# One store of 8 KB blocks for all phases of a hybrid decoder layer, bulk transfers on a second queue

## The chip, the core and the metric

One core of a Trainium2 chip runs the whole layer. The metric is the device time of one execution in microseconds (us).

## The reference

One layer over 2048 tokens of width 1024, float32. Cut to what matters:

```python
u = h @ w_in
q, k, v, xr, gr = jnp.split(u, splits, axis=-1)
att = sliding_window_sink_attention(q, k, v, attn_sinks)   # window 128
xr = causal_dwconv(xr, rnn_conv_w, rnn_conv_b)
rec = rg_lru(xr, gate_a_w, gate_a_b, gate_x_w, gate_x_b, lru_lambda)
rec = rec * jax.nn.gelu(gr, approximate=True)
mix = jnp.concatenate([att, rec], axis=-1) @ w_out
h = layer_norm(ALPHA * h + mix, ln1_g, ln1_b)
gate, val = jnp.split(h @ w_up, 2, axis=-1)               # 1024 -> 2 x 3072
gate = causal_dwconv(gate, conv_w, conv_b)
ffn = (jax.nn.gelu(gate, approximate=True) * val) @ w_down
ple = jax.nn.sigmoid(h @ ple_gate_w + ple_gate_b) * (p @ ple_proj)
h = layer_norm(ALPHA * h + ffn + ple, ln2_g, ln2_b)
```

## The kernel before

Every product is made of three: each operand is split into a high and a low part in a 32-bit matmul type (`split_sb`, lines 111 to 113: ACT copies the high part, DVE subtracts), and `mm3` (lines 129 to 132) issues hi x hi, hi x lo and lo x hi. So nearly all time of PE has lines 130 to 132. Weights come as units of 128 x 1024 words (512 KB) through `wst` (3 buffers) and are split into `wb` (8 buffers of half a unit).

*Phase A* (lines 230 to 572) runs over 4 chunks of 512 tokens. x of a chunk is split into four tiles of the pool `t1` (4 buffers of 8 KB a partition). The first stage (`first_stage`) makes 14 units of 128 columns from it; then come RG-LRU, attention, and the mixing with W_OUT into four tiles of 128 tokens, norm 1 (`layer_norm`), and PE transposes that give h as `hh_`, `hl_` (again the four buffers of `t1`) and `hf` (pool `t2`). The gating of the per-layer embedding (lines 542 to 571) then makes, in two halves `dh` of 512 columns, four tiles of 24 matmuls each with h, and DVE adds the result into `rs`, which is stored to DRAM as `rsd`. The next chunk's x needs the buffers that gating still reads.

*Between the phases.* Two chunks form a half `s2` for the FFN. Up uses a scheme with seven products in place of eight, on operands B11, T2, B21, T1, T3, T4, B22 (`HX`), each 4 x 128 x 512 in two parts, 2 MB. An even chunk stores its h as B11, B21 and `hfd`; an odd chunk stores B22, and `combine` (lines 518 to 532) reads `hfd` back, makes T1 to T4 by four adds and four splits for each of four slices, and stores 8 pieces of 256 KB a slice. All four calls stand in the first half of gating, one behind each token tile. All these pass through DRAM (`hxd`).

*Up* (lines 581 to 670, twice) closes phase A's pools, opens its own, and loads all seven operands (line 595). Then 24 feature tiles `ft` run `begin`, `middle`, `end`, with the order of PE written out by hand; the results gc go to DRAM (`gd`), two feature tiles a block. *Down* (lines 672 to 722, twice) opens its own pools again and runs over two chunks; for each of 12 steps `kp` it loads `graw`, splits it into `gb`, and adds 2 x 4 token tiles x 6 matmuls into eight PSUM banks; after the last step come the sums with `rsd`, norm 2 and the store of four token tiles.

*What sets the order.* A scheduler orders the instructions of each engine, except where `order(...)` or the manual schedule of up pins them. Pools opened with `scoped` (`reuse_waits="tile"`) share memory between phases, and a tile of a new phase waits for the old tiles at its place. Every DMA is issued on SP's queue. Where the tiles of phase A start follows from what was allocated before them: `t1`, `t2` and pt tiles lie 96 bytes past a multiple of 128, the attention's and gates' temporaries 32 past; all of up and down and `wb` lie at a multiple of 128.

## Time and profile before

| what | value |
|---|---|
| median of 3 runs | 2465.29 us (2464.33 to 2469.13) |
| the profiled execution, its own time | 2466.69 us |
| span in the profile | 2465.0 us |
| PE busy | 2329.7 us, 95%, 10156 matmuls |
| DVE, ACT, POOL busy | 67%, 44%, 6% |
| phase A; up, down of half 0; up, down of half 1 | to 938; 1422, 1690; 2182, 2465 us |
| DMA | 340.08 MB, nearly all on one queue |

A view by windows gives, for a stretch of the span, each engine's busy time and count of instructions, the granted clock of TensorE as a share of its full level (2.4 GHz; the lower level is 1.2), and what the DMA engines did. Matmuls overlap, so a count in a window says more than a mean duration. The waits say how long PE stood still and what released it.

### The profile page before, as it was taken

How to read it: one execution, taken by the hardware profiler on the slowest of the kernel's cores; microseconds unless marked ns; L12 is line 12 of the kernel's file. 1: busy time of each engine (PE TensorE's matmuls, PEld its weight loads, DVE VectorE, ACT ScalarE, POOL GpSimd, SP SyncE). 2: the span in 40 equal slices, each digit the busy share in tenths (PEclk: the TensorE clock that was granted, in tenths of full speed). 3: DMA queues.
4: the chain of work that ended last, by engine and by line, in shares of the span. 5: the costliest groups of instructions: out<-in, count | busy, mean ns of one | idle time of the engine just before them, and what ended most of it. 6: DMA issues, size and time to landing. Idle time of an engine off the chain costs nothing. (4 is left out here: it accounts for less than half of the span.)

```text
span 2465.0 us, 28138 instructions
## 1 busy us (share of the span) xinstructions
PE 2329.7 (95%) x10156; PEld 1882.5 (76%) x10156; DVE 1657.6 (67%) x2728; ACT 1084.1 (44%) x2028; POOL 145.7 (6%) x258
## 2 busy tenths in 40 slices
PE   9999999799989987999999999996999999999997
PEld 7777777577777765888888878884788888878886
DVE  7975788678668773877777743635677777753634
ACT  7643665466446452444444433331344444433331
POOL 1300030003002100000000000000000000000000
PEclk9999999899999998999999999998999999999999
DMA  4236325732542287232222264635422222264551
GB/s 160 90 131 236 111 69 194 249 111 77 195 156 94 94 282 298 94 91 81 86 77 86 94 227 140 220 122 197 179 83 88 86 77 79 92 214 141 182 173 60
DMA packets 99308, 340.08 MB, mean 138 GB/s; under 512 B 10464, under 2 KB 10592, under 8 KB 93536
## 3 DMA queue, kind: packets, MB, share of 16 engines
q1 hardware_dynamic: 99168, 338.28, 40.4%
q8 instruction: 80, 1.31, 0.2%
q14 instruction: 60, 0.49, 0.1%
HBM read 262.74 MB, written 75.50 MB: 137 GB/s over the span
## 5 line engine op out<-in xcount | busy, mean ns | idle before, releaser
L112 ACT CAST wb<-wst 128x512 fp32r<-128x512 f32 x640 | 390.6, 621 | 741.5 <-PE sc L132 286.5
L113 DVE TENSOR_TENSOR wb<-wst,wb 128x512 fp32r<-128x512 f32 x640 | 433.5, 686 | 322.9 <-ACT wb L112 321.7
L131 PE MATMUL b<-T,wb 128*128 128x512 f32 x576 | 225.4, 391 | 2.8 <-DMA T<-hxT 2.8
L130 PE MATMUL b<-T,wb 128*128 128x512 f32 x576 | 225.7, 392 | 2.2 <-DVE u L642 1.6
L132 PE MATMUL b<-T,wb 128*128 128x512 f32 x576 | 224.9, 391 | 0.4 <-DVE wb L113 0.4
L601 DVE SCALAR_TENSOR_TENSOR gc<-xb,prm,gc 128x512 f32<-128x512 f32 x192 | 144.1, 750 | 109.9 <-issue 84.4
L130 PE MATMUL a<-B,wb 128*128 128x512 f32 x384 | 151.8, 395 | 29.6 <-DMA B<-hxB 29.6
L112 ACT CAST wb<-s 128x512 fp32r<-128x512 f32 x144 | 89.4, 621 | 195.0 <-PE a L132 92.6
L131 PE MATMUL a<-B,wb 128*128 128x512 f32 x384 | 152.4, 397 | 6.8 <-DMA B<-hxB 6.8
L132 PE MATMUL a<-B,wb 128*128 128x512 f32 x384 | 151.6, 395 | 0.0
L113 DVE TENSOR_TENSOR wb<-s,wb 128x512 fp32r<-128x512 f32 x144 | 99.3, 689 | 62.1 <-ACT wb L112 62.1
L131 PEld LDWEIGHTS b<-T,wb 128*128 128x128 f32 x576 | 108.7, 189 | 27.1 <-DMA T<-hxT 4.9
L130 PEld LDWEIGHTS b<-T,wb 128*128 128x128 f32 x576 | 108.8, 189 | 26.6 <-DVE u L642 2.7
L132 PEld LDWEIGHTS b<-T,wb 128*128 128x128 f32 x576 | 108.6, 189 | 23.3 <-DVE wb L113 0.8
L130 PE MATMUL acc<-wb,t1h 128*128 128x512 f32 x256 | 104.1, 415 | 20.2 <-ACT wb L112 14.2
L130 PEld LDWEIGHTS a<-B,wb 128*128 128x128 f32 x384 | 73.5, 191 | 46.0 <-issue 30.6
L132 PE MATMUL acc<-wb,t1l 128*128 128x512 f32 x256 | 103.6, 406 | 1.2 <-DVE t1l L88 1.2
L131 PE MATMUL acc<-wb,t1h 128*128 128x512 f32 x256 | 104.5, 409 | 0.0
L130 PE MATMUL acc<-t1h,wb 128*128 128x512 f32 x192 | 81.2, 423 | 23.4 <-ACT wb L112 23.1
L132 PE MATMUL a<-t1h,wb 128*128 128x512 f32 x256 | 102.7, 401 | 0.0
L130 PE MATMUL a<-t1h,wb 128*128 128x512 f32 x256 | 102.6, 401 | 0.0
L131 PE MATMUL a<-t1l,wb 128*128 128x512 f32 x256 | 102.4, 400 | 0.0
(246 smaller groups left out, 5564.1 us busy)
## 6 DMA issues: line engine op xcount, KB each, us to landing
wst<-in_w_dram SPq DMA_DIRECT2D x319, 512.0 KB, 3.7
gd<-gc SPq DMA_DIRECT2D x48, 512.0 KB, 4.8
...
T<-hxT SPq DMA_DIRECT2D x16, 1024.0 KB, 19.6
...
```

What stands on the lines that cost most here:

```text
L112: ACT.copy(hi, src)
L113: (eng or DVE).tensor_tensor(lo, src, f(hi), ALU.subtract)
L130: order(PE.matmul(o, ah, bh, start=first, stop=False, skip_group_check=more), after)
L131: PE.matmul(o, ah, bl, start=False, stop=False, skip_group_check=more)
L132: return PE.matmul(o, al, bh, start=False, stop=last, skip_group_check=more)
L601: DVE.scalar_tensor_tensor(gc, xb[:, o:o + T], pc(C_FW + 3 * ft + t_), gc, ALU.mult, ALU.add)
```

## The change

All tiles of 8 KB a partition (k and v, gate weights, x, m, q, h, hf, pt, the operands of up, graw, gb) come from one pool `h` of 13 blocks, and no pool is closed before the end. Temporaries share tags over all phases (`xc` 3, `xd` 1, `r` 4, others 2), rows with a conv tail come from `row()` (2 buffers). `epst` is 9 columns wide and the pools are so ordered that every TensorE operand starts at a multiple of 128 bytes. The stores of `hxd`, `hfd` and `rsd` and the loads of `hx` go to POOL's queue. The seven operands of up(0) are asked for in chunk 3: B11 after the last scores, T2 and B21 after mixing, T1, T3, T4 after gating's first half, B22 at its end, B22's low part into four pieces in `pch`/`pcl`. Those of up(1) are asked for in down(0)'s second chunk, four after step 6 and three at the end. Two combines stand in each half of gating. The x loads of the next chunk are ordered after the transposes. Up stores each 512-column half of gc by itself, with a row each; `graw` holds two steps. In down the last two steps run token tile by token tile; norms of tiles 0 and 1 (all four in the last chunk) follow their sums at once, those of 2 and 3 are put off into the next phase (`later`). The diff, cut to its core:

```diff
+XB = T + 8
+N8 = 13
...
+    h_p = ctx.enter_context(tc.tile_pool(name="h", bufs=N8))
+    tmp = ctx.enter_context(tc.tile_pool(name="tmp", bufs=2))
+    xb_p = ctx.enter_context(tc.tile_pool(name="xb", bufs=2))
...
+    def h8(name, shape, dt=F32R):
+        return h_p.tile(shape, dt, tag="h", name=nm(name))
...
-    epst = cst.tile([P, 1], F32, tag="epst", name="epst")
+    epst = cst.tile([P, 9], F32, tag="epst", name="epst")[:, 0:1]
...
+    def load_hx(s2, names, earlier):
+        for n in names:
+            hx[s2][n] = []
+            for m in range(2):
+                if (n, m) == (HX[-1], 1):
+                    ts = [tm(("pch", "pcl")[k % 2], F32R) for k in range(4)]
+                    for k in range(4):
+                        order(POOL.dma_start(f(ts[k]), hxd[s2][n][:, m, k, :]), earlier)
+                else:
+                    t = h8(n, [P, 4, T])
+                    order(POOL.dma_start(f(t), hxd[s2][n][:, m]), earlier)
+                    ts = [t[:, k, :] for k in range(4)]
+                hx[s2][n].append(ts)
...
-            SP.dma_start(st.rearrange("p (k t) -> p k t", k=2), xt[c, :, 2 * u:2 * u + 2, :])
+            order(SP.dma_start(st.rearrange("p (k t) -> p k t", k=2), xt[c, :, 2 * u:2 * u + 2, :]), have_h)
...
+        if c == NCH - 1:
+            load_hx(0, HX[:1], last_scores)
+            load_hx(0, HX[1:3], [mixed])
...
-                    SP.dma_start(hxd[s2][n][:, m], f(t))
-                SP.dma_start(hfd[s2][:, 4 * u:4 * u + 4], hf[u])
+                    POOL.dma_start(hxd[s2][n][:, m], f(t))
+                POOL.dma_start(hfd[s2][:, 4 * u:4 * u + 4], hf[u])
...
-                SP.dma_start(hxd[s2][n][:, 0, kt, :], f(hi))
-                SP.dma_start(hxd[s2][n][:, 1, kt, :], f(lo))
+                POOL.dma_start(hxd[s2][n][:, 0, kt, :], f(hi))
+                POOL.dma_start(hxd[s2][n][:, 1, kt, :], f(lo))
...
-                    SP.dma_start(rsd[c * NTOK + t_], rs[t_])
-                elif c % 2:
-                    combine(t_)
+                    POOL.dma_start(rsd[c * NTOK + t_], rs[t_])
+                if c % 2 and t_ % 2 != dh:
+                    combine(2 * dh + t_ // 2)
+            if dh == 0:
+                half = [gated]
+        if c == NCH - 1:
+            load_hx(0, HX[3:6], half)
+            load_hx(0, HX[6:], [gated])
...
-            for n in HX:
-                for m in range(2):
-                    SP.dma_start(f(hx[n][:, m]), hxd[s2][n][:, m])
...
-                SP.dma_start(gd[s2][ft // 2][:, ft % 2, :], gc)
+            SP.dma_start(o[:, 0:T], v["gc"])
+            product(v["C"], w3, x["B22"], False)
+            xb = row()
+            POOL.tensor_copy(xb[:, 0:2], gtail[:, ft, :])
...
+            SP.dma_start(o[:, T:2 * T], gc)
...
+            v = begin(0)
+            middle(v)
+            while later:
+                later.pop(0)()
...
-                accs = [[bank(tag) for _ in range(2)] for tag in ("a", "b", "acc", "sc")]
+            accs = [[bank(tag) for _ in range(2)] for tag in ("sc", "a", "b", "acc")]
...
+                    if c == 1:
+                        load_hx(1, HX[:4], marks[-1:])
...
+            for t_ in range(NTOK):
+                for kp, dh in wbs:
+                    i = sums(kp, t_, dh, gbs[kp], wbs[kp, dh])
+                for dh in range(2):
+                    d = rs[t_][:, dh * 512:(dh + 1) * 512]
+                    DVE.tensor_tensor(d, d, accs[t_][dh], ALU.add)
+                if c == NCH - 1 or t_ < 2:
+                    norm(t_)
...
+            if c == 1:
+                load_hx(1, HX[4:], marks[-2:-1])
+            if c < NCH - 1:
+                def rest(norm=norm):
+                    fence()
+                    norm(2)
+                    norm(3)
+                    fence()
+                later.append(rest)
```

**DVE at the seam of chunks 0 and 1.** Before (`t1l` is the low part of the next x, `P` and `r` are the gating of a token tile, the last lines of chunk 0):

```order
L563 TENSOR_TENSOR P_2108<-acc_2083,ln_1742 128x512
L565 TENSOR_TENSOR P_2108<-P_2108,ph_1978 128x512
L567 SCALAR_TENSOR_TENSOR r_1346<-r_1346,P_2108 128x512
L113 TENSOR_TENSOR t1l_2147<-wst_2149,t1h_2145 128x1024
L113 TENSOR_TENSOR t1l_2147<-wst_2153,t1h_2145 128x1024
L563 TENSOR_TENSOR P_2139<-acc_2114,ln_1742 128x512
L113 TENSOR_TENSOR t1l_2148<-wst_2157,t1h_2146 128x1024
L565 TENSOR_TENSOR P_2139<-P_2139,pl_1987 128x512
L567 SCALAR_TENSOR_TENSOR r_1348<-r_1348,P_2139 128x512
L113 TENSOR_TENSOR t1l_2148<-wst_2161,t1h_2146 128x1024
```

After (`xl` is the low part of the next x, line 588 opens the gating of a tile):

```order
L124 TENSOR_TENSOR xl_2124<-wst_2126,xh_2122 128x1024
L124 TENSOR_TENSOR wb_1992<-wst_1990,wb_1992 128x512
L124 TENSOR_TENSOR wb_1995<-wst_1990,wb_1995 128x512
L124 TENSOR_TENSOR xl_2124<-wst_2130,xh_2122 128x1024
L588 TENSOR_TENSOR P_2023<-acc_1998,ln_1719 128x512
L124 TENSOR_TENSOR xl_2125<-wst_2134,xh_2123 128x1024
L590 TENSOR_TENSOR P_2023<-P_2023,ph_1937 128x512
L124 TENSOR_TENSOR xl_2125<-wst_2138,xh_2123 128x1024
L592 SCALAR_TENSOR_TENSOR r_1319<-r_1319,P_2023 128x512
L588 TENSOR_TENSOR P_2054<-acc_2029,ln_1719 128x512
L590 TENSOR_TENSOR P_2054<-P_2054,pl_1946 128x512
```

`r_1319` is the row tile of token tile 0 and `r_1348` that of tile 3: the four x splits now stand beside the gating of the first token tile, where before they stand beside that of the last.

**The queue that loads up(0)'s operands.** Before, on SP, the end of chunk 3:

```order
L569 DMA rsd13_99<-r_1358_7268 128x1024
L569 DMA rsd14_100<-r_1359_7270 128x1024
L569 DMA rsd15_101<-r_1360_7272 128x1024
L595 DMA B11_1542_8220<-hxB11_0_128 128x2048 x2
L595 DMA T2_1543_8221<-hxT2_0_129 128x2048 x2
L595 DMA B21_1544_8222<-hxB21_0_130 128x2048 x2
L595 DMA T1_1545_8223<-hxT1_0_131 128x2048 x2
L595 DMA T3_1546_8224<-hxT3_0_132 128x2048 x2
L595 DMA T4_1547_8225<-hxT4_0_133 128x2048 x2
L595 DMA B22_1548_8226<-hxB22_0_134 128x2048 x2
L122 DMA wst_1571_8356<-in_w_dram 128x1024
```

After, on POOL (the first three operands stand 40 rows earlier in this queue, T1 between combine's stores):

```order
L557 DMA hxT4_1_144<-pcl_1548_8162 128x512
L594 DMA rsd15_117<-r_1363_7249 128x1024
L249 DMA T3_1553_8202<-hxT3_0_136 128x2048
L249 DMA T3_1554_8204<-hxT3_0_136 128x2048
L249 DMA T4_1555_8206<-hxT4_0_137 128x2048
L249 DMA T4_1556_8208<-hxT4_0_137 128x2048
L249 DMA B22_1557_8210<-hxB22_0_138 128x2048
L246 DMA pch_1558_8212<-hxB22_0_138 128x512
L246 DMA pcl_1559_8213<-hxB22_0_138 128x512
L246 DMA pch_1560_8214<-hxB22_0_138 128x512
L246 DMA pcl_1561_8215<-hxB22_0_138 128x512
L654 COPY xb_1579_8297<-gtail_100 128x2
```

The loads of the last three operands stand behind the last `rsd` store in either queue; weights are no longer in that queue.

**PE where up(0) ends and down(0) begins.** After (`sc` is down's first accumulator, T_1555 and T_1556 are T4, acc_11743 takes B22; before, the first product with gb stands behind the last of up):

```order
L142 MATMUL b_11742<-T_1554_8204,wb_11678 128x512
L143 MATMUL b_11742<-T_1553_8202,wb_11678 128x512
L141 MATMUL sc_11851<-wb_11868,gb_11861 128x512
L142 MATMUL sc_11851<-wb_11868,gb_11861 128x512
L143 MATMUL sc_11851<-wb_11868,gb_11861 128x512
L141 MATMUL sc_11851<-wb_11871,gb_11861 128x512
L141 MATMUL b_11742<-T_1555_8206,wb_11681 128x512
L142 MATMUL b_11742<-T_1556_8208,wb_11681 128x512
```

Four matmuls of down now stand ahead of up's last two products.

## Rows read from the trace of the kernel before

**Rows 1.** The page: busy time, share of the span and instructions of each engine.

```profile
PE 2329.7 (95%) x10156; PEld 1882.5 (76%) x10156; DVE 1657.6 (67%) x2728; ACT 1084.1 (44%) x2028; POOL 145.7 (6%) x258
```

**Rows 2.** Windows without a wait of PE: us, busy (x count) by engine, granted clock, DMA share, GB/s.

```profile
480.00:526.00 46.00, 46.00 (x199) 37.00 (x198) 28.47 (x45) 31.89 (x52) 1.52 (x6) 1.00 0.35 115
...
652.00:696.00 44.00, 44.00 (x189) 35.36 (x188) 22.32 (x33) 14.18 (x24) 0.00 (x0) 1.00 0.62 227
...
1000.00:1400.00 400.00, 400.00 (x1766) 331.34 (x1765) 300.13 (x464) 167.68 (x275) 18.71 (x42) 1.00 0.27 85
...
1440.00:1690.00 250.00, 250.00 (x1104) 207.01 (x1103) 115.35 (x183) 79.79 (x140) 0.00 (x0) 1.00 0.47 157
```

**Rows 3.** Windows, same columns: seams, odd gatings, starts of up and down, the end.

```profile
225.00:245.00 20.00, 13.90 (x49) 10.70 (x48) 13.71 (x18) 11.16 (x17) 0.18 (x1) 0.83 0.74 240
...
426.00:486.00 60.00, 44.76 (x159) 33.15 (x158) 39.61 (x60) 26.00 (x44) 0.39 (x3) 0.83 0.77 266
...
694.00:714.00 20.00, 13.80 (x48) 10.61 (x47) 13.82 (x19) 11.09 (x17) 0.18 (x1) 0.74 0.76 262
...
862.00:938.00 76.00, 65.75 (x266) 49.73 (x265) 54.59 (x86) 37.80 (x67) 0.00 (x0) 0.91 0.73 252
...
890.00:938.00 48.00, 38.27 (x138) 28.50 (x137) 30.78 (x49) 18.25 (x32) 0.00 (x0) 0.86 0.73 256
...
938.00:988.00 50.00, 32.03 (x109) 23.01 (x108) 18.55 (x29) 12.05 (x21) 0.66 (x2) 0.80 0.82 332
...
1414.00:1434.00 20.00, 14.84 (x54) 11.28 (x53) 11.92 (x19) 7.08 (x13) 0.93 (x3) 0.83 0.66 221
...
1688.00:1744.00 56.00, 29.25 (x101) 21.21 (x100) 27.67 (x44) 10.79 (x19) 0.00 (x0) 0.76 0.81 326
...
2174.00:2194.00 20.00, 14.84 (x58) 11.35 (x57) 11.92 (x19) 7.50 (x14) 0.10 (x1) 0.91 0.67 222
...
2449.90:2465.00 15.10, 0.00 (x0) 0.00 (x0) 11.32 (x17) 0.88 (x3) 0.00 (x0) 0.60 0.35 139
```

**Rows 4.** Waits of PE: us in total, times, longest us.

```profile
PE acc L130 <- ACT wb L112: 37.3, 8, 6.2
...
PE a L130 <- DMA B<-hxB: 29.6, 2, 19.6
...
PE a L130 <- ACT gb L112: 8.7, 2, 4.4
```

**Rows 5.** Lines of DVE in 400:440: names, shapes, count, busy us, mean ns, idle before.

```profile
L113 DVE TENSOR_TENSOR pcl<-xc,pch 128x512 fp32r<-128x512 f32 x12 | 7.9, 686 | 0.8 <-ACT pch L112 0.8
...
L563 DVE TENSOR_TENSOR P<-acc,ln 128x512 f32<-128x512 f32 x4 | 2.7, 686 | 0.2 <-PE acc L132 0.2
```

**Rows 6.** Timeline of DVE and SP at the end: start us, us, instruction.

```profile
2454.78 0.63 DVE L714 TENSOR_TENSOR r<-r,sc 128x512 f32<-128x512 f32 x1
...
2456.59 0.68 DVE L197 BATCH_NORM_STATS2 st<-r 128x6 f32<-128x512 f32 x1
...
2458.38 0.20 DVE L199 BATCH_NORM_AGGREGATE mv<-st 128x2 f32<-128x12 f32 x1
...
2459.81 0.16 DVE L202 RECIPROCAL rs<-rs 128x1 f32<-128x1 f32 x1
...
2460.01 1.28 DVE L204 SCALAR_TENSOR_TENSOR r<-r,rs,ln 128x1024 f32<-128x1024 f32 x1
...
2461.32 0.81 SPq L719 DMA_DIRECT2D out_dram<-r  x2
```

**Rows 7.** DMA: durations of issues (min/median/max ns), and us from issue to landing.

```profile
L595 SPq DMA_DIRECT2D T<-hxT x16: 319/355/822, 943.5 to 1718.4; - x16
...
DMA to landing us min/median/max: 6.1/18.5/20.8
...
L531 SPq DMA_DIRECT2D hxT<-pch x32: 319/320/936, 412.4 to 915.8; - x32
```

**Rows 8.** Lines of POOL, its longest mean.

```profile
L353 POOL COPY htail<-xc 128x1 f32<-128x1 f32 x16 | 19.0, 1186 | 105.5 <-DVE xc L352 104.8
```

More of the change, by code (lines that the diff above doesn't have):

```diff
@@ L239, in x_flat, with t_pair @@
+    for c in range(NCH):
+        def t_pair(name):
+            return [[h8(name + m, [P, 4, T]) for _ in range(2)] for m in "hl"]
+        xh, xl = t_pair("x")
         def x_flat(u):
@@ L355 @@
         ACT.copy(vt, pv)
-        qs_ = [t2_p.tile([P, 4, T], F32R, tag="t2", name=nm("q")) for _ in range(2)]
+        qs_ = [h8("q", [P, 4, T]) for _ in range(2)]
         for j in range(4):
@@ new lines, in up, with conv, begin @@
+        x = hx[s2]
+        def conv(gc, src, xb, ft):
+            ACT.activation(gc, src, AF.Identity, bias=pc(C_FB + ft), scale=pc(C_FW + 3 * ft + 2))
+            for t_ in (1, 0):
+                DVE.scalar_tensor_tensor(gc, xb[:, t_:t_ + T], pc(C_FW + 3 * ft + t_), gc, ALU.mult, ALU.add)
+            act(gc, gc, AF.Gelu_apprx_tanh)
+        def begin(ft):
+            rg, rv = wraw(W_UP + 2 * ft), wraw(W_UP + 2 * ft + 1)
+            a11, a12, a21, a22 = rg[:, 0:512], rg[:, 512:1024], rv[:, 0:512], rv[:, 512:1024]
+            s1, s2_, s4 = tm("xc"), tm("xc"), tm("xc")
+            DVE.tensor_tensor(s1, a21, a22, ALU.add)
+            w1 = wblock(a11)
+            DVE.tensor_tensor(s2_, s1, a11, ALU.subtract)
+            w6 = wblock(s2_)
+            w2 = wblock(a12)
+            w5 = wblock(s1)
+            DVE.tensor_tensor(a21, a11, a21, ALU.subtract)
+            w7 = wblock(a21)
+            w4 = wblock(a22)
+            DVE.tensor_tensor(s4, a12, s2_, ALU.subtract)
+            w3 = wblock(s4)
+            v = dict(ft=ft, w=(w1, w2, w3, w4, w5, w6, w7))
+            v["A"] = bank("a")
+            product(v["A"], w1, x["B11"], True)
+            v["p1"] = tm("P")
+            ACT.copy(v["p1"], v["A"])
+            return v
@@ new lines, in middle @@
+        def middle(v):
+            ft, (w1, w2, w3, w4, w5, w6, w7) = v["ft"], v["w"]
+            p1 = v["p1"]
+            v["B"], v["C"] = bank("b"), bank("acc")
+            product(v["B"], w6, x["T2"], True)
+            v["u2"] = tm("ph")
+            DVE.tensor_tensor(v["u2"], v["B"], p1, ALU.add)
+            product(v["A"], w2, x["B21"], False)
+            xb = row()
+            POOL.tensor_copy(xb[:, 0:2], gtail[:, ft, :])
+            ACT.copy(xb[:, 2:2 + T], v["A"])
+            POOL.tensor_copy(gtail[:, ft, :], xb[:, T:T + 2])
+            v["gc"] = tm("pl")
+            conv(v["gc"], v["A"], xb, ft)
+            product(v["C"], w5, x["T1"], True)
+            product(v["B"], w7, x["T3"], False)
+            u3 = tm("xd")
+            DVE.tensor_tensor(u3, v["B"], p1, ALU.add)
+            v["val"] = tm("ph")
+            DVE.tensor_tensor(v["val"], v["C"], u3, ALU.add)
@@ new lines, in end @@
+        def end(v):
+            ft, (w1, w2, w3, w4, w5, w6, w7) = v["ft"], v["w"]
+            o = gd[s2][ft // 4][:, ft % 4, :]
+            product(v["B"], w4, x["T4"], False)
+            v1 = tm("xd")
+            DVE.tensor_tensor(v1, v["B"], v["p1"], ALU.add)
+            DVE.tensor_tensor(v["gc"], v["gc"], v1, ALU.mult)
+            SP.dma_start(o[:, 0:T], v["gc"])
+            product(v["C"], w3, x["B22"], False)
+            xb = row()
+            POOL.tensor_copy(xb[:, 0:2], gtail[:, ft, :])
+            g2 = xb[:, 2:2 + T]
+            DVE.tensor_tensor(g2, v["C"], v["u2"], ALU.add)
+            if s2 == 0:
+                POOL.tensor_copy(gtail[:, ft, :], xb[:, T:T + 2])
+            gc = tm("r", cols=1024)[:, 0:T]
+            conv(gc, g2, xb, ft)
+            DVE.tensor_tensor(gc, gc, v["val"], ALU.mult)
+            SP.dma_start(o[:, T:2 * T], gc)
```

280 lines of the change are left out of this document (105 added, 175 removed).

## The prediction

> **What bounds the kernel now.** I read the page's busy line first: PE is busy 95% of the span, DVE 67%, POOL 6% [rows 1]. So the time is PE's, and a gain can only come from matmuls that stand closer together or from holes between them. The windows view of stretches in which PE never waits gives the first kind [rows 2]. In each the count is one more than the steps between starts, since a matmul that straddles an edge is counted. Up and down step by 400/1765 = 0.2266 us and 250/1103 = 0.2267 us a matmul. Phase A, with the same 128x512 shape, steps by 44/188 = 0.2340 in chunk 2's gating and by 46/198 = 0.2323 us in its first stage, at a granted clock of 1.00 like the others. That is 5.7 to 7.3 ns a matmul that the second half of the kernel doesn't pay.
>
> The holes are in the windows around the seams [rows 3]. What a window loses is its length less (count - 1) steps: 20 - 48 x 0.234 = 8.8 us at the seam of chunks 0 and 1; 60 - 158 x 0.234 = 23.0 in chunk 1's gating with its seam; 20 - 47 x 0.234 = 9.0 at the seam of chunks 2 and 3; 48 - 137 x 0.234 = 15.9 in chunk 3's gating; 50 - 108 x 0.2267 = 25.5 where up(0) begins; 7.1 where down(0) begins (its 54 matmuls have the PE time of the 58 at down(1), so I count 58 and take records as missing); 56 - 100 x 0.2267 = 33.3 where up(1) begins; 7.1 where down(1) begins; 15.1 behind the last matmul. Together 144.8 us. The granted clock is 0.74 to 0.91 in all of them (0.60 at the end, where PE is idle), so a share of each hole is matmuls at 1.2 GHz after PE stood still, and it goes with the hole.
>
> The chain of waits says who ends the holes [rows 4]: casts of weights on ACT (37.3 us in 8 waits, behind x casts that need a block still held), the loads of B11 at the two starts of up (29.6 us in 2 waits), and gb's first cast (8.7 us in 2).
>
> **The change, part by part.**
>
> *Alignment.* The code's 512-column matmuls of a chunk are 336 in the first stage, 192 + 192 + 48 in W_OUT, gate and PLE projection, and 56 in gates and attention. If steps fall to those of up: 336 x 5.7 + 432 x 7.2 + 56 x 6 ns = 5.4 us a chunk, **-21.5 us** in four. Bounds 0 and -24 (824 x 7.3 ns x 4). I take the upper part, since gb, hx and wb start at multiples of 128 bytes before, phase A's tiles don't, and shape and clock are the same. The Trainium skill, page "SBUF — State Buffer", section "Operand start alignment", asks for a start at a multiple of the element and calls that a matter of legality, not of speed; by it this term is 0, and the rows' difference has another cause (rival 1).
>
> *Seams of chunks 0/1 and 2/3.* Next chunk's x blocks no longer wait for hh/hl of the last: the order of DVE has the xl splits beside the first tile's gating, not the last's. What is late next is PE's own end of the chunk. **-16** of 17.8; bounds 0 and -17.8.
>
> *Chunk 1's gating and its seam.* Before, DVE owes the first half four combines of 8 x 0.69 us [rows 5] = 22, four gatings of 3 x 0.69 = 8.3, and 10 weight splits = 6.9: 37 us beside 120 matmuls x 0.234 = 28 us of PE. After, two combines stand in each half: 26 us of 27 (at the new step). The second half adds four x splits of 128x1024, priced as the 1.28 us row of that size [rows 6]: 5 us too much, and stores that must land before pch/pcl come free. I keep 7 of 23.0: **-16**; bounds -4 and -23.
>
> *Chunk 3's gating and up(0)'s start.* The same spread, and B11, T2, B21 are asked for before gating, T1 in its middle, T3, T4, B22 on POOL's queue behind the last rsd store, as POOL's order shows. Before, the 28 such loads of both phases landed a median 18.5 us after issue, all of a phase being asked for at once [rows 7]. Moved ahead they meet the stores of gating: from the end of mixing to up(0), 862 to 938, DMA already moves 76 us x 252 GB/s = 19 MB [rows 3]; T2, B21 and T1 add 6, and at the 332 GB/s of up(0)'s start the 76 us hold 25. It fits barely. T3, T4 and B22 are first read 4, 6 and 7 products into up(0), 12 x 0.227 = 2.7 us each, so at 10.9, 16.3 and 19.1 us, and their 6 MB at 332 GB/s take 18 us: they arrive as they are read. I keep 13 of 41.4: **-28**; bounds -10 and -41.
>
> *Down(0) and down(1) begin.* The PE order interleaves the first sc products with the last products of up, and blocks for graw and gb come free when B11 was read last, eight products before up's end. **-6.5 and -6** of 7.1 each; bounds 0 and -7.1.
>
> *Up(1) begins.* Four tensors of hx are loaded in the middle of down(0)'s second chunk, where DMA moves 157 GB/s in 250 us [rows 2], so 8 MB find room; T3 to B22 follow at its end, and T3 is read 10.9 us after. Norms of t2 and t3 move behind the first middle of up(1): 2 x 5.5 us of DVE, in a phase where DVE is busy 300 of 400 us [rows 2], so 100 us cover it; without cover it would hold the gating of ft 0. **-31** of 33.3; bounds -15 and -33.
>
> *The end.* Before, 15.1 us stand behind the last matmul: four tiles' sums and norms in DVE's order, then 3.7 us from the last DVE row's end to the span's end [rows 6]. After, only the last tile's last half add (0.63), bn_stats (0.68), aggregate and reciprocal (0.36), two 1.28 us steps and the 3.7 us remain: 7.9, and a tile's DVE work of 2 x 0.63 + 2 x 0.68 + 0.36 + 2.56 = 5.5 us equals the 24 x 0.227 = 5.45 us of its PE work, so DVE lags by about 1. **-6**; bounds -3 and -7.5.
>
> *At nothing.* Twice the gd stores (48 more of 256 KB on SP) and POOL copies (two more a feature tile, 0.24 to 0.63 us) in up: POOL is busy 18.7 of 400 us there [rows 2]. Half as many graw loads, of 1 MB. PE's products are the same 10156 instructions.
>
> *The second queue.* No row shows a DMA issued by POOL. From below it costs what an SP issue does, 0.32 to 0.94 us [rows 7]; from above the longest mean of POOL's own groups, 1.19 us [rows 8]. POOL's order has 38 such issues at chunk 1's gating and 55 from chunk 3's mixing to its end: 55 x 1.19 = 65 us beside 54, 38 x 1.19 = 45. I take 0.94 us (the top of what that row has for these very stores): 52 and 36 us, hidden behind gating, with nothing to spare in chunk 3.
>
> **Sum.** -21.5 - 16 - 16 - 28 - 6.5 - 6 - 31 - 6 = -131. The profiled execution has a span of 2465.0 and a time of 2466.69 us, 1.7 outside the span, 1.4 above the median of 2465.29. 2465.0 - 131 + 1.7 - 1.4 = **2334 us**.
>
> **The rivals.**
>
> 1. *Alignment is worth nothing*: phase A's steps are longer because ACT, DVE and POOL read and write beside PE there. For it: no row separates the two. Against it: DVE is busy 300 of 400 us in up, more than in 652:696 (22 of 44), and up's step is the short one [rows 2]. 2334 + 21.5 = 2355.5.
>
> 2. *The bulk on POOL's queue is late.* The order has hx loads of 1 MB ahead of combine's stores in one queue; pch and pcl have two buffers, so DVE's next split waits for landings, and DVE's order holds gating behind it. Then chunk 1 gains nothing and chunk 3 half: 2334 + 16 + 18 = 2368. For it: DMA share is 0.77 and 0.73 in those windows already [rows 3]. Against it: combines come half as densely.
>
> 3. *Slower than before.* POOL's issues themselves become the bound of the odd chunks' gating. At p us each they add 55p - 54 and 38p - 54; the forecast's gain of 131 is gone from p = 2.6 us. An issue that stood back for four DVE instructions of 0.69 us would cost 2.76: 98 + 51 = +149, 2483 us. For it: DVE would run 26 of 27 us there. Against it: POOL's own groups take at most 1.19 us in the mean beside the same DVE [rows 8]. The Trainium skill, "SBUF — State Buffer", section "SBUF: two separate sides", has it that a DVE instruction on the shared port keeps GpSimd from writing descriptors and gives about 3.1 us for a DMA so held; its sum would be 55 x 3.1 - 54 + 38 x 3.1 - 54 = 180 us more, an estimate from that page, 2514.
>
> 4. *The loads are asked for early and land late all the same*, since no block is free or 25 MB don't fit. Then up(0)'s start keeps its 25.5 and up(1)'s half of 31: 2334 + 12 + 15 = 2361, and with rival 2 about 2379.
>
> **How the numbers follow.** Forecast 0.65, rival 1 0.15, rival 2 0.10, rival 4 0.06, rival 3 0.04. Upwards the range takes rivals 1, 2 and most of 4 and leaves out rival 3 and pairs of rivals: 2372. Downwards all of what I kept at the seams, 1.8 + 7 + 13.4 + 2.3 us, could go as well: 2309.5, and 2308 with the last of the alignment. A measurement of this kernel tells about 0.2% (5 us) from no change. All cases but rival 3 are faster; 2 in 100 is left for a sum of mishaps that ends level.
>
> **What would show it.** Right: steps of 0.227 us in stretches like those of [rows 2] in phase A; under 3 us lost at the seams of chunks 0/1 and 2/3; no wait of PE on a load of B11 or on gb; under 10 us behind the last matmul. Wrong: steps of 0.234 in phase A (rival 1); waits on pch or pcl landings in gating (rival 2); POOL's issues over 2 us and end to end in gating (rival 3); waits of over 5 us on hx loads in up(0) or up(1) (rival 4).

## The result, and the profile after

| what | before | after |
|---|---|---|
| median, us (range) | 2467.21 (2464.33 to 2469.14), 4 runs beside those of the change | 2377.59 (2377.13 to 2380.04), 4 runs |
| span of the profiled execution, us | 2465.0 | 2375.4 |
| first matmul of up(0), us | 948.9 | 915.1 |

The ratio is 0.964 (95% interval 0.9623 to 0.9656): 89.6 us less where 131 were forecast, and 5.6 us above the upper end of the range. The page of the changed kernel: PE's busy line, the DMA queue on which POOL issues, and the issue of the T operands of up, 1 MB each.

```profile
PE 2291.5 (96%) x10156; PEld 1871.1 (79%) x10156; DVE 1653.0 (70%) x2728; ACT 1084.5 (46%) x2030; POOL 265.2 (11%) x483
...
q0 software_dynamic: 14112, 71.31, 7.6%
...
T<-hxT POOLq DMA_DIRECT2D x16, 1024.0 KB, 9.8
```

PE is busy for most of the span as before [rows 1], with 38 us less of busy time; POOL has 225 more instructions, and 71 MB go through its queue. Those loads now land a median 9.8 us after their issue, where they took 18.5 [rows 7].

The windows of the changed kernel answer to [rows 2] and [rows 3]. Columns: us, busy (x count) of PE, PEld, DVE, ACT, POOL, then granted clock, DMA share, GB/s. In order: two stretches of phase A and one of up(0) without a wait of PE, and then the places where holes were: chunk 0's embedding products, the seam of chunks 0 and 1, chunk 1's gating and seam, the seam of 2 and 3, the first 30 us of chunk 3's gating in three pieces, the way from the end of mixing to up(0), up(0)'s start, the starts of down(0), up(1) and down(1), and the end.

```profile
650.00:720.00 70.00, 70.00 (x310) 57.93 (x310) 44.79 (x67) 42.72 (x68) 3.90 (x10) 1.00 0.45 152
1000.00:1370.00 370.00, 370.00 (x1634) 306.39 (x1633) 271.44 (x421) 153.48 (x251) 31.30 (x77) 1.00 0.28 87
190.00:215.00 25.00, 21.31 (x82) 17.08 (x81) 12.92 (x19) 11.85 (x19) 0.00 (x0) 0.86 0.68 243
220.00:240.00 20.00, 20.00 (x90) 16.56 (x89) 12.87 (x21) 9.27 (x16) 1.78 (x4) 1.00 0.67 234
408.00:468.00 60.00, 49.30 (x196) 38.40 (x195) 46.41 (x72) 29.77 (x50) 18.33 (x35) 0.91 0.84 299
664.00:684.00 20.00, 20.00 (x90) 16.57 (x89) 13.82 (x22) 9.38 (x16) 1.86 (x5) 1.00 0.64 234
828.00:838.00 10.00, 5.68 (x31) 3.92 (x29) 6.94 (x12) 3.96 (x8) 0.54 (x1) 0.97 1.02 422
838.00:848.00 10.00, 9.10 (x36) 7.12 (x37) 5.16 (x7) 5.80 (x11) 0.00 (x0) 0.69 0.39 136
848.00:858.00 10.00, 2.11 (x6) 0.88 (x4) 6.56 (x10) 3.28 (x6) 3.23 (x6) 0.65 0.97 366
828.00:915.00 87.00, 68.72 (x274) 52.73 (x273) 55.75 (x88) 37.44 (x67) 19.47 (x37) 0.86 0.73 273
915.00:950.00 35.00, 26.38 (x101) 20.57 (x101) 21.61 (x36) 12.53 (x22) 8.83 (x17) 0.85 0.83 320
1375.00:1395.00 20.00, 20.00 (x89) 16.33 (x88) 14.09 (x22) 8.20 (x14) 3.53 (x4) 1.00 0.79 262
1640.00:1660.00 20.00, 20.00 (x90) 16.57 (x89) 19.62 (x33) 7.91 (x14) 1.79 (x4) 1.00 0.57 214
2096.00:2116.00 20.00, 19.58 (x86) 15.87 (x85) 13.97 (x22) 8.16 (x15) 2.39 (x2) 1.00 0.75 264
2366.70:2375.40 8.70, 0.00 (x0) 0.00 (x0) 4.67 (x7) 0.29 (x1) 0.00 (x0) 0.69 0.30 121
```

Read as the prediction reads them, length less (count - 1) steps. Phase A now steps by 70/309 = 0.2265 us, as up does (370/1633 = 0.2266). The seams of chunks 0/1 and 2/3 and the starts of down(0) and up(1) lose nothing (90 matmuls in 20 us are 89 x 0.2267 = 20.2), down(1)'s loses 0.7. Chunk 1's window still loses 60 - 195 x 0.2267 = 15.8 us. Where up(0) starts 35 - 100 x 0.2267 = 12.3 are lost, of 25.5 before, but from the end of mixing to up(0) now 87 - 273 x 0.2267 = 25.1. And there is a new hole of 25 - 81 x 0.2267 = 6.6 in chunk 0's embedding products; before, 190 to 220 us had no wait of PE.

The waits of PE in the changed kernel: us in total, times, longest.

```profile
PE acc L141 <- ACT wb L123: 12.0, 3, 5.4
...
PE a L141 <- ACT ph L577: 6.1, 3, 3.7
...
PE b L141 <- DMA T<-hxT: 5.4, 1, 5.4
PE a L141 <- ACT pt L123: 4.7, 1, 4.7
PE acc L143 <- DVE wb L124: 3.8, 1, 3.8
PE a L143 <- DVE pt L124: 3.7, 1, 3.7
```

Against [rows 4]: waits on casts of weights are 12.0 us instead of 37.3, those on B11 (29.6) and on gb's first cast (8.7) are gone but for 1.2 us; new are two on `pt` (the embedding operand of a chunk) in chunk 3, three on `ph` (an embedding result that ACT copies out of PSUM: 3.7 us in chunk 0, 1.7 in chunk 2, 0.7 in chunk 3), and 5.4 us on a T block in up(0).

The end on DVE's timeline (start us, us, instruction), which answers to [rows 6]:

```profile
2367.16 0.67 DVE L766 TENSOR_TENSOR r<-r,acc 128x512 f32<-128x512 f32 x1
2367.86 0.69 DVE L214 BATCH_NORM_STATS2 st<-r 128x6 f32<-128x512 f32 x1
...
2370.23 1.28 DVE L221 SCALAR_TENSOR_TENSOR r<-r,rs,ln 128x1024 f32<-128x1024 f32 x1
```

One half add, one half's statistics and the norm of one tile stand there, and the span ends 3.9 us behind the last row's end: 8.7 us behind the last matmul instead of 15.1.

### The profile page after: what moved, and what is told of

It reads as the page before. It is cut to its first block, busy times and chain, and to the rows that moved or that the text cites. A ratio compares the mean times of both kernels' runs of the same rounds, so it can differ in the third digit from the quotient of the medians.

```text
span 2375.4 us, 28589 instructions
## 1 busy us (share of the span) xinstructions
PE 2291.5 (96%) x10156; PEld 1871.1 (79%) x10156; DVE 1653.0 (70%) x2728; ACT 1084.5 (46%) x2030; POOL 265.2 (11%) x483
## 4 chain that ended last, share of the span: by engine, by line
PE 59%; DVE 2%; DMA 1%; ACT 0%; issue 0%; DVEq 0%; ACTq 0%
PE b L141 7%; PE b L143 7%; PE b L142 7%; PE acc L141 5%; PE acc L143 5%; PE acc L142 5%; PE a L141 5%; PE a L143 5%; PE a L142 5%; PE sc L143 2%; PE sc L142 2%; PE sc L141 2%; DMA wst<-in_w_dram 1%; DMA xb<-hfd 0%; DVE st L214 0%
## 5 line engine op out<-in xcount | busy, mean ns | idle before, releaser
L123 ACT CAST wb<-xc 128x512 fp32r<-128x512 f32 x144 | 89.4, 621 | 199.1 <-PE a L143 94.5
L141 PE MATMUL a<-B,wb 128*128 128x512 f32 x384 | 149.6, 390 | 0.0
L142 PE MATMUL a<-B,wb 128*128 128x512 f32 x384 | 149.5, 389 | 0.0
L143 PE MATMUL a<-B,wb 128*128 128x512 f32 x384 | 149.4, 389 | 0.0
L124 DVE TENSOR_TENSOR wb<-xc,wb 128x512 fp32r<-128x512 f32 x144 | 99.1, 688 | 50.8 <-ACT wb L123 50.8
L620 DVE SCALAR_TENSOR_TENSOR pl<-xb,prm,pl 128x512 f32<-128x512 f32 x96 | 71.8, 748 | 78.7 <-POOL xb L676 77.4
L141 PE MATMUL acc<-wb,hh 128*128 128x512 f32 x256 | 101.5, 401 | 11.4 <-DVE P L588 5.8
L143 PE MATMUL acc<-wb,hl 128*128 128x512 f32 x256 | 101.7, 399 | 1.7 <-DVE hl L99 1.7
L142 PE MATMUL acc<-wb,hh 128*128 128x512 f32 x256 | 102.3, 400 | 0.0
L142 PE MATMUL a<-xl,wb 128*128 128x512 f32 x256 | 101.0, 394 | 0.0
L141 PE MATMUL a<-xh,wb 128*128 128x512 f32 x256 | 100.7, 393 | 0.0
L143 PE MATMUL a<-xh,wb 128*128 128x512 f32 x256 | 100.6, 393 | 0.0
L141 PE MATMUL acc<-xh,wb 128*128 128x512 f32 x192 | 77.5, 403 | 8.0 <-ACT wb L123 7.5
L143 PEld LDWEIGHTS a<-B,wb 128*128 128x128 f32 x384 | 72.2, 188 | 15.1
```

The source lines that it names most:

```text
L123: ACT.copy(hi, src)
L124: (eng or DVE).tensor_tensor(lo, src, f(hi), ALU.subtract)
L141: order(PE.matmul(o, ah, bh, start=first, stop=False, skip_group_check=more), after)
L142: PE.matmul(o, ah, bl, start=False, stop=False, skip_group_check=more)
L143: return PE.matmul(o, al, bh, start=False, stop=last, skip_group_check=more)
L620: DVE.scalar_tensor_tensor(gc, xb[:, t_:t_ + T], pc(C_FW + 3 * ft + t_), gc, ALU.mult, ALU.add)
```

## The experiments: where chunk 3's gain went

The term that failed most is chunk 3's gating with up(0)'s start. In that stretch the changed kernel issues three loads of 1 MB (T2's second part and both parts of B21) between 825.7 and 828.4 us, on POOL's queue, when mixing ends:

```profile
825.72 0.54 POOL L249 DMA_DIRECT2D T<-hxT  x1 [38.84 <-PE acc L143]
```

The brackets hold POOL's idle time before that issue and what ended it. T2's first part had gone out at 786.34; the second stood 38.8 us at the head of the queue until PE's mixing products were done, and B21 stood behind it. ACT then waits for a unit of weights:

```profile
838.20 0.62 ACT L123 CAST wb<-wst 128x512 fp32r<-128x512 f32 x1 [4.86 <-DMA wst<-in_w_dram]
...
851.48 1.14 ACT L123 CAST pch<-xc 128x512 fp32r<-128x512 f32 x2 [2.02 <-DVE xc L551]
852.52 1.04 ACT L123 CAST pt<-wst 128x1024 fp32r<-128x1024 f32 x1
```

The second wait is of another kind: the cast of `pt` stands behind two casts of combine's (`pch`), which wait for DVE's adds, and these for hh and hf of the transposed h. Theory 1: the early loads share the DMA engines with the weights and delay them. Theory 2: combine's casts ahead of pt are the cause, and the loads do no harm. Four kernels tell them apart.

**late_loads.** T2 and B21 are asked for one by one, each behind a gating token tile of chunk 3's first half. (`order` only sets the place in the order of issue; POOL doesn't wait for PE by it. In the trace T2's two loads go out together at 846.8 us and B21's at 855.4 and 864.2, between stores of combine's that POOL has to wait for.)

```diff
-            load_hx(0, HX[1:3], [mixed])
+            pend = []
+            for n in HX[1:3]:
...
+                    t = h8(n, [P, 4, T])
+                    pend.append((t, n, m))
...
+                if c == NCH - 1 and dh == 0:
+                    t, n, m = pend[t_]
+                    order(POOL.dma_start(f(t), hxd[0][n][:, m]), [gated])
```

> Chunk 3 of the changed kernel loses 23 us between 834 and 885. Theory 1 (the burst: T2's second part and B21, 3 to 4 MB asked for when mixing ends, fill the DMA engines, and the weight loads of W_OUT's end and the gate come late): with these loads asked for one behind each token tile of gating's first half, PE's wait on the weight cast at 834 (4.5 us) and its time at 1.2 GHz behind it are gone; 2362 to 2368 us. Theory 2 (the order: combine's adds and casts stand ahead of the split of the per-layer embedding on DVE and ACT): the two waits at 848 and 854 stay, 2372 to 2378 us.

Measured: 2362.58 us (2356.08 to 2364.67), ratio 0.9575 (0.9561 to 0.9589), 15 us below the change. First the loads of weights that SP issues from 825.7 to 833.2 us, in the changed kernel, with the time from issue to landing (min/median/max):

```profile
L133 SPq DMA_DIRECT2D wst<-in_w_dram x3: 328/328/328, 825.8 to 833.2; - x3
...
DMA to landing us min/median/max: 3.5/6.2/8.1
```

The same with late_loads:

```profile
L133 SPq DMA_DIRECT2D wst<-in_w_dram x3: 328/328/328, 825.7 to 833.1; - x3
...
DMA to landing us min/median/max: 3.4/3.5/3.6
```

and ACT's timeline of late_loads at the same place:

```profile
833.59 0.62 ACT L123 CAST wb<-wst 128x512 fp32r<-128x512 f32 x1 [0.26 <-DMA wst<-in_w_dram]
...
836.89 1.06 ACT L123 CAST pt<-wst 128x1024 fp32r<-128x1024 f32 x1
...
845.33 0.62 ACT L123 CAST pch<-xc 128x512 fp32r<-128x512 f32 x1
```

The same three loads, issued at the same times, land up to 4.5 us sooner, and the cast that came at 838.20 comes at 833.59. The DMA engines of the changed kernel moved 422 GB/s at a share of 1.02 from 828 to 838. But the edit did a second thing: the scheduler's order on ACT changed with it. In the changed kernel the cast of pt stands behind the first casts of pch (851.48, then 852.52); with late_loads it stands ahead of them (836.89, then 845.33). So the 15 us are the loads and the order of ACT together, and the next two kernels split them.

**pinned_combine.** The loads as in the change; combine's first two adds on DVE are ordered behind the token tile's matmuls.

```diff
-        def combine(kt):
+        def combine(kt, after):
...
-            DVE.tensor_tensor(t3, b22, b12, ALU.subtract)
-            DVE.tensor_tensor(t1, b12, b11, ALU.subtract)
+            order(DVE.tensor_tensor(t3, b22, b12, ALU.subtract), after)
+            order(DVE.tensor_tensor(t1, b12, b11, ALU.subtract), after)
```

> Only the first adds of each combine are ordered behind the last matmul of the token tile they are written after. Theory 2 (the order): the waits of PE on the embedding's cast and split (4.7 and 3.7 us) and the time at 1.2 GHz behind them go, 2360 to 2367 us. Theory 1 (the burst): these waits are short without them too, but the weight cast's wait at 834 stays and others take the place of those gone; 2372 to 2378 us.

**late_pinned.** Both edits.

> Both edits. If theory 1 alone holds it is as fast as the late loads alone, if theory 2 alone as the pinned combine alone; if each has its own part, 2350 to 2360 us, with the loads then later for up(0), whose start may lose up to 5 us more than the 12 of the changed kernel.

Measured: pinned_combine 2371.33 us (2370.06 to 2375.28), ratio 0.9618 (0.9603 to 0.9632); late_pinned 2363.79 us (2363.35 to 2364.42), ratio 0.9584 (0.957 to 0.9599). The window from the end of mixing for 87 us, in late_loads:

```profile
828.00:915.00 87.00, 75.60 (x322) 58.24 (x320) 68.25 (x109) 46.06 (x82) 26.88 (x50) 0.96 0.90 333
```

in pinned_combine:

```profile
828.00:915.00 87.00, 71.70 (x281) 54.97 (x280) 55.96 (x90) 38.70 (x69) 19.99 (x38) 0.89 0.75 272
```

With the order pinned the cast of pt costs PE 1.6 us instead of 4.7, while the wait on the weights stays (4.3 us, at 834.99): 6 us are gained (all four runs lie below all four of the change, though the intervals of the ratios touch). The time lies between the ranges of the two theories. Taking the loads out of the way as well gives 7.5 more, and pinning gains nothing on top of late_loads. By its expectation that would speak for theory 1 alone, but late_loads already has pt ahead of pch, so there was little left to pin. The starts of stretches on PE's timeline (us) show where each gain arises:

| kernel | chunk 3's gating | up(0) | down(0) | gating to down(0) |
|---|---|---|---|---|
| the change | 829.5 | 915.1 | 1379.0 | 549.5 |
| pinned_combine | 825.8 | 906.0 | 1372.9 | 547.1 |
| late_loads | 829.5 | 895.4 | 1364.2 | 534.7 |
| late_pinned | 826.3 | 896.1 | 1364.7 | 538.4 |

So both theories hold a part, and the loads, which share the DMA engines with the weights, the larger one. With the order pinned, moving the loads is worth 8.7 us in this stretch. Pinning with the loads left in place is worth 2.4; the other 3.7 us of pinned_combine were gained before chunk 3's gating begins. What is left of late_loads' 14.8 was not separated. In the changed kernel the windows from 838 to 858 have a granted clock of 0.69 and 0.65, which lies between the lower level of 1.2 GHz (0.5) and full speed: each of these waits is followed by matmuls at the lower level. With late_loads the whole 87 us have 0.96, and up(0) begins 19.7 us sooner; 15 of those reach down(0) and the end. Of the rest, 3.0 us go to a new wait on a cast of weights at 901.2, and the waits on T blocks in up(0) are 6.6 and 2.4 us, against 5.4 and 1.9 in the change.

**no_prefetch0.** If the early loads do harm, none might do better: all seven operands of up(0) are asked for behind gating.

```diff
-            load_hx(0, HX[:1], last_scores)
-            load_hx(0, HX[1:3], [mixed])
...
-            load_hx(0, HX[3:6], half)
-            load_hx(0, HX[6:], [gated])
+            load_hx(0, HX, [gated])
```

> The loads of up(0)'s operands all stand behind gating, as the kernel before has them. If the early loads are worth their collisions, up(0)'s start loses 25 us as before and chunk 3's gating gains most of its 23 back: 2372 to 2384 us. If the early loads carried the gain that the prediction put on them (28 us), 2395 to 2405 us.

Measured: 2376.19 us (2371.94 to 2382.57), ratio 0.9645 (0.9626 to 0.9663), no different from the change. The profiled execution is the slowest of its four. Its windows of gating and of up(0)'s start:

```profile
820.00:905.00 85.00, 76.73 (x340) 61.02 (x339) 70.33 (x112) 42.58 (x79) 19.36 (x36) 0.98 0.65 231
905.00:955.00 50.00, 27.81 (x96) 20.37 (x97) 20.85 (x33) 10.52 (x18) 12.53 (x23) 0.76 0.94 380
```

Up to 905 us gating loses 85 - 339 x 0.2267 = 8.1 us, and up(0)'s start loses 50 - 95 x 0.2267 = 28.5 with 12.4 and 7.3 us of waits on loads of B blocks. What the early loads gave at up(0) they took in gating: as they are placed in the change their net worth is zero.

**bulk_on_sp.** Every transfer that went to POOL's queue goes to SP's again.

```diff
-                        order(POOL.dma_start(f(ts[k]), hxd[s2][n][:, m, k, :]), earlier)
+                        order(SP.dma_start(f(ts[k]), hxd[s2][n][:, m, k, :]), earlier)
...
-                POOL.dma_start(hxd[s2][n][:, 0, kt, :], f(hi))
+                SP.dma_start(hxd[s2][n][:, 0, kt, :], f(hi))
```

> All transfers of the changed kernel that POOL issues go back to SP's queue. Theory 1 (the DMA engines are shared, whichever queue asks): the weights stand behind the bulk in one queue, 2377 to 2400 us. Rival (the queue of POOL itself is slow or takes more than its share): 2350 to 2372 us.

Measured: 2384.07 us (2382.52 to 2385.95), ratio 0.9668 (0.9652 to 0.9684), 6.5 us above the change. The waits of PE:

```profile
PE b L141 <- ACT wb L123: 27.5, 1, 27.5
PE acc L141 <- ACT wb L123: 23.2, 4, 13.2
```

The 13.2 us stand at chunk 1's seam and the 27.5 in up(0): on SP the weights now stand behind bulk transfers that themselves wait for a block or for DVE. Since the whole costs only 6.5, other waits went: chunk 3's way from gating to up(0) takes 73.6 us instead of 85.6, and chunk 0 has no hole (below). The second queue is worth that much here, far from what the two waits alone would say. What POOL pays for an issue, from the changed kernel (min/median/max ns), for combine's stores and for the loads of up's operands:

```profile
L556 POOL DMA_DIRECT2D hxT<-pch x32: 539/539/547, 403.3 to 916.9; - x32
...
DMA to landing us min/median/max: 2.3/4.7/7.7
```

```profile
L249 POOL DMA_DIRECT2D T<-hxT x16: 537/538/548, 786.3 to 1645.4; - x16
```

It is 0.54 us each. That is the issue alone: POOL also stands idle ahead of some, for a block or a split (38.8 us ahead of T2's second part), and what stands behind waits with it.

**late_spread.** late_loads, and in even chunks the six stores of 1 MB one behind each of six gating tiles, to see whether that burst makes the hole at 199 us of chunk 0.

```diff
         if c % 2 == 0:
+            bulk = []
...
-                    POOL.dma_start(hxd[s2][n][:, m], f(t))
-                POOL.dma_start(hfd[s2][:, 4 * u:4 * u + 4], hf[u])
+                    bulk.append((hxd[s2][n][:, m], f(t)))
...
+                if c % 2 == 0 and 4 * dh + t_ < 6:
+                    order(POOL.dma_start(*bulk[4 * dh + t_]), [gated])
```

> The late loads, and in the even chunks the six stores of 1 MB one behind each of six token tiles of gating, where the changed kernel asks for all six at once. Theory 1 (a burst on one queue delays the weights on the other): PE's waits at the second half's embedding products of chunks 0 and 2 go, 2355 to 2361 us. Rival (these waits come from weights that PE now uses up faster, burst or not): 2361 to 2365 us.

Measured: 2359.27 us (2358.76 to 2361.78), ratio 0.9575 (0.9561 to 0.9589), the same ratio as late_loads. The wait on `ph` in chunk 0 stays (1.9 us, at 201.96), and that in chunk 2 is gone. But the burst was hardly spread:

```profile
181.44 0.53 POOL L595 DMA_DIRECT2D hxB<-hh  x1
...
217.03 0.53 POOL L595 DMA_DIRECT2D hxB<-hl  x1
```

Five of the six stores still go out between 178.95 and 181.97 us, where the change issues all six from 176.83 to 181.02. `order` gave them later places, but POOL had nothing to wait for. So this kernel doesn't tell whether the burst makes the hole. The changed kernel's trace shows what PE waits for: ACT's copy of `ph` stands behind a cast of weights that waits for their landing.

```profile
202.24 0.62 ACT L123 CAST wb<-wst 128x512 fp32r<-128x512 f32 x1 [3.71 <-DMA wst<-in_w_dram]
202.76 0.58 ACT L577 COPY ph<-a 128x512 f32<-128x512 f32 x1
```

In shifted_after and late_loads, whose chunk 0 has the same code, the wait is 1.7 us and not 3.7. In bulk_on_sp the six stores go out as close together (176.4 to 182.8 us), but ACT copies `ph` at 198.32, ahead of the casts of weights, and the same window has no wait:

```profile
190.00:215.00 25.00, 25.00 (x112) 20.71 (x111) 16.70 (x23) 13.44 (x21) 0.00 (x0) 1.00 0.68 224
```

That is chunk 3's second cause again, the place of a small copy in ACT's order; how much the burst adds stays open. late_spread has the lowest median of all kernels here, 18 us below the change, though not to be told from late_loads.

**v2 and v3.** T3 still makes PE wait 8.9 us in late_spread's up(0). v2 asks for T3 and T4 ahead of the last combine and of the last two stores of `rsd`; v3 also takes the copies of the conv tail of the first two feature tiles from POOL to DVE.

```diff
-            load_hx(0, HX[3:6], half)
+            load_hx(0, HX[3:4], half)
+            load_hx(0, HX[4:6], [gated])
+            for t_ in range(2, NTOK):
+                POOL.dma_start(rsd[c * NTOK + t_], rs[t_])
+            combine(3)
...
-            POOL.tensor_copy(xb[:, 0:2], gtail[:, ft, :])
+            (DVE if s2 == 0 and ft < 2 else POOL).tensor_copy(xb[:, 0:2], gtail[:, ft, :])
```

> As the one before, and in chunk 3 the last combine and the last two rsd stores stand behind the loads of T3 and T4 on POOL's queue. If these loads are late because they are asked for behind the last store of gating, up(0)'s start loses 4 to 7 us in place of 13: 2350 to 2356 us. If the DMA engines are full there anyway: 2357 to 2363 us.

> The kernel with late loads, spread stores and T3, T4 ahead of the last stores lost 12.8 us in one wait at up(0)'s start, on DVE's row behind two copies that POOL issues after the loads of B22. With these copies on DVE for the first two feature tiles of up(0): that wait is under 4 us, 2348 to 2356 us. Rival (the DMA engines are full there and the next load is what PE waits for): 2357 to 2362 us.

Measured: v2 2361.13 us (2360.28 to 2366.92), ratio 0.9588 (0.9572 to 0.9604); v3 2362.53 us (2359.41 to 2365.19), ratio 0.9586 (0.9572 to 0.9601). No gain. The wait on T3 is gone and another stands in its place, in v2 (13.7 us in v3):

```profile
PE b L141 <- DVE xd L679: 12.9, 2, 12.7
```

`xd` has one buffer, and up's use of it (line 679) stands on DVE behind the last combine's split of `xd`: at 923.5 and 924.2 us in v2, at 925.4 and 926.6 in v3. In v2 DVE stood 6.3 us, up to 920.25, for a unit of weights to land ahead of that split. That the moved loads made it late is argued and not shown. The tail copies on POOL were not the cause.

## The experiments: what the alignment did

**aligned_before.** The kernel before with a spare tile of 32 bytes and rows of T + 32, so that every TensorE operand starts at a multiple of 128 bytes, and nothing else changed.

```diff
+    gap = a_p.tile([P, 8], F32, tag="gap", name="gap")
+    POOL.memset(gap, 0.0)
...
-            xb = tm("xb", cols=3 + T)
+            xb = tm("xb", cols=T + 32)
...
-            ACT.copy(xb[:, 3:], px)
+            ACT.copy(xb[:, 3:3 + T], px)
```

> The kernel before with one unused tile of 32 bytes and longer rows, so that every TensorE operand starts at a multiple of 128 bytes and nothing else changes. If the start alone sets the step: 0.227 us a matmul in phase A and 18 to 24 us less than before, 2443 to 2449 us. Rival 1 of the prediction (the longer step comes from what runs beside PE): 2464 to 2469 us.

Measured: 2463.11 us (2459.71 to 2468.74), with 2465.85 for the kernel before beside it, ratio 0.9993 (0.9983 to 1.0002). Two windows of phase A without a wait of PE:

```profile
490.00:520.00 30.00, 30.00 (x130) 24.32 (x130) 18.29 (x29) 21.60 (x35) 0.93 (x3) 1.00 0.29 88
...
656.00:686.00 30.00, 30.00 (x130) 24.12 (x130) 14.59 (x22) 10.06 (x18) 0.00 (x0) 1.00 0.57 198
```

Both step by 30/129 = 0.2326 us. Multiples of 128 bytes bought nothing, as rival 1 has it.

**shifted_after.** The other side: the change with `epst` one column wide again, so that all operands lie 96 bytes past a multiple of 128.

```diff
-    epst = cst.tile([P, 9], F32, tag="epst", name="epst")[:, 0:1]
+    epst = cst.tile([P, 1], F32, tag="epst", name="epst")
```

> The changed kernel with the constant of 9 columns back at 1, so that all its operands, those of up and down and the weights too, start 96 bytes past a multiple of 128. If the start alone sets the step, all of some 9700 matmuls of 512 columns cost 5.7 to 7.3 ns more: 2433 to 2449 us. Rival 1: within 4 us of 2378.

Measured: 2376.68 us (2375.09 to 2379.71), ratio 0.9645 (0.9631 to 0.966), the same as the change. Where an operand starts by itself doesn't matter. What the two kernels differ in is how far the streamed operand and the loaded one lie apart: in aligned_before x and h lie 128 bytes past a multiple of 256 from `wb`, in shifted_after a multiple of 256 like everything in the change. Theory: that distance sets the step, and the other engines' work doesn't.

**before_same_256.** aligned_before with a spare tile of 160 bytes instead of 32: the distance from wb to x, h and the mixing operands is a multiple of 256.

```diff
-    gap = a_p.tile([P, 8], F32, tag="gap", name="gap")
+    gap = a_p.tile([P, 40], F32, tag="gap", name="gap")
```

> The kernel before with an unused tile of 160 bytes and longer rows, so that x, h and the mixing's tiles lie a multiple of 256 bytes from the weights, where before they lie 96 past one and in the aligned kernel 128 past one. New theory (the step hangs on the distance of the two operands modulo 256 bytes, 0 in up and down of every run and in all of the changed kernel): 0.227 us a matmul in phase A and 18 to 24 us less than before, 2442 to 2448 us. Rival (the distance is not it, something else in phase A of the old kernel is): 2459 to 2467 us with steps of 0.232 to 0.234.

**after_off_128.** The change with the small tiles' pool (1152 bytes) opened between wb and the 8 KB blocks, so that all blocks lie 128 past a multiple of 256 from wb.

```diff
     wb_p = ctx.enter_context(tc.tile_pool(name="wb", bufs=8))
+    sml = ctx.enter_context(tc.tile_pool(name="sml", bufs=4))
     h_p = ctx.enter_context(tc.tile_pool(name="h", bufs=N8))
...
-    sml = ctx.enter_context(tc.tile_pool(name="sml", bufs=4))
```

> The changed kernel with the pool of small tiles (1152 bytes) opened between the weights and the 8 KB blocks, so that all blocks lie 128 past a multiple of 256 bytes from the weights, each of them still at a multiple of 128. New theory: steps of 0.2324 to 0.2333 us as in phase A of the aligned kernel, now in all some 9700 matmuls of 512 columns, 55 to 65 us more: 2433 to 2443 us. Rival: 2375 to 2382 us.

Measured: before_same_256 2451.69 us (2447.52 to 2453.5), ratio 0.9946 (0.9932 to 0.9961), 13.1 us below the 2464.78 of the kernel before beside it. Its first stage:

```profile
475.00:519.00 44.00, 44.00 (x196) 36.47 (x195) 28.57 (x45) 31.88 (x52) 1.52 (x6) 1.00 0.36 115
```

after_off_128 2420.95 us (2419.91 to 2421.42), ratio 0.9823 (0.9806 to 0.9839), 43 us above the change; the windows that the changed kernel ran in 0.2265 and 0.2266 us a matmul:

```profile
656.00:726.00 70.00, 70.00 (x303) 56.84 (x302) 43.89 (x66) 41.17 (x66) 3.90 (x10) 1.00 0.47 153
1000.00:1370.00 370.00, 370.00 (x1594) 300.41 (x1593) 268.45 (x418) 150.76 (x247) 35.96 (x76) 1.00 0.26 82
```

70/302 = 0.2318 and 370/1593 = 0.2323 us, with the same DVE, ACT and POOL work beside PE, and 44/195 = 0.2256 in before_same_256. So the distance sets the step, in both kernels and both ways: 5.7 ns a matmul in up. For the some 6400 products of up and down that is 36 of the 43 us, which leaves 7 for phase A.

## Why the prediction was right or wrong

By its own windows, its terms came out as follows; the row for alignment is what is left of the 89.6 us between the spans.

| term | forecast, us | measured, us | how |
|---|---|---|---|
| alignment | -21.5 | -14 | remainder; 13.1 when done alone, 7 when undone in phase A |
| seams 0/1 and 2/3 | -16 | -11.2 | 17.8 gone, 6.6 new in chunk 0 |
| chunk 1's gating and seam | -16 | -7.2 | 15.8 kept of 23.0 |
| chunk 3's gating, up(0)'s start | -28 | -4.0 | 25.1 + 12.3 kept of 41.4 |
| down(0), down(1) begin | -12.5 | -13.5 | 0 and 0.7 kept |
| up(1) begins | -31 | -33.3 | 0 kept |
| the end | -6 | -6.4 | 8.7 of 15.1 kept |

**The step that failed** is "Chunk 3's gating and up(0)'s start": it kept 13 of the 41.4 us and found 37.4, below its own least gain of 10. From chunk 3's first gating product to up(0)'s first it is 85.6 us where it was 86.1, and up(0)'s next 120 products take 39.6 where they took 42.7. Its working asked whether 25 MB fit in the 76 us, and they do on the mean. It didn't ask when they are moved: T2's second part and B21 come in one burst at the end of mixing, when a block comes free, just as gating asks for its weights, and the weights' landing goes from 3.5 to as much as 8.1 us, with only three buffers of units to cover it. Behind that the cast of pt stood behind combine's casts in ACT's order, which the prediction had not read at that place (it read DVE, POOL and SP). late_loads, pinned_combine and late_pinned put 15 us on these two, of the 24 that the term missed. Of the rest, 7.3 us are two waits on T3 in up(0): the prediction had T3, T4 and B22 arrive as they are read, but T3's loads go out at 920.0, 4.9 us after up(0)'s first product, behind the last store of `rsd`. The Trainium skill, page "DMA: Bandwidth & Descriptors", section "Issuing engines are not separate DMA queues", says that transfers issued by different engines run on the same 16 DMA engines and interleave; the rows of late_loads agree, with 3.5 against 6.2 us in the median for the same three loads.

**Rival 4** had up(0)'s start keep its 25.5 us. It kept 12.3, so the early loads did arrive; no_prefetch0 shows the same time with 28.5 lost at that place. But T2's second part found no block free, as this rival has it, and PE's 5.4 us on a T block just meet its sign of over 5. None of the four rivals has a load that delays something else, and the range ended 5.6 us too low.

**Alignment.** The size was off by 7 us or more, and the reason was wrong. The bounds (0 and -24) hold it, and phase A's steps did fall to those of up. But rival 1 was right that multiples of 128 are worth nothing (aligned_before), and wrong that the other engines make phase A's steps long (after_off_128, before_same_256). The forecast came near because the same edit also put every operand at a multiple of 256 bytes from wb. Phase A's shorter steps would give some 20 us if all of them reached the end; that its waits swallow the rest is argued and not shown.

**Seams 0/1 and 2/3** were right at their place: nothing is lost there. The forecast called "PE's own end of the chunk" next late; chunk 0 lost 6.6 us ahead of it, at a wait on ACT's copy of `ph` behind a late cast of weights.

**Chunk 1** kept 15.8 us instead of 7. PE's waits there are 0.9, 1.9, 1.5, 2.1 and 3.8 us, on splits of weights and on gating's adds by ACT and DVE, none on a load into `h`. DVE is busy 46.4 of 60 us there, so the estimate of 26 of 27 us was not exceeded as a sum. But ACT waits for a store of `pch` to land, and the casts of weights that PE waits 2.1 us for stand behind that wait:

```profile
450.99 0.62 ACT L123 CAST pch<-xc 128x512 fp32r<-128x512 f32 x1 [3.67 <-DMA hxT<-pch]
...
452.78 1.14 ACT L123 CAST wb<-wst 128x512 fp32r<-128x512 f32 x2
```

That the order in which ACT and DVE serve splits and combines makes the other waits is argued. pinned_combine, which also moves combine's adds in chunk 1, takes 227.9 us from this chunk's gating to chunk 2's, against 228.8.

**Down and up(1)** went as argued: the loads in the middle of down(0), the interleaved first products and the graw blocks that come free early leave no wait over 1.3 us at any of the three starts. The hole before down(0) was 8.0 us and not 7.1: no records are missing there, all 10156 products are in the trace; 12 of them step by 0.43 us, at the lower clock. **The end** too: 8.7 against 9.1.

**Rival 3** fell by the price: 0.54 us an issue in place of the 0.94 taken and far from the 2.6 that it needs. The Trainium skill, "SBUF — State Buffer", section "SBUF: two separate sides", has a DVE instruction on the shared port hold back GpSimd's descriptors; with DVE busy 46.4 of 60 us in chunk 1's gating none of combine's 64 issues took POOL over 549 ns. No row here shows such a hold. **Rival 2** is half right in its outcome (chunk 1 gained 7 of 16), and its sign shows: the wait of 3.7 us on a landing of `pch` above, and 2.6 us of DVE's on one of `pcl` at 443.56. How much of chunk 1's loss it makes was not measured. (Its sum takes 18 us for half of chunk 3's 28; half is 14, which gives 2364.)
